# A planner that allows each weight load more time, job orders searched anew, and layer 1's rotary products on VectorE

## The chip, the cores and the metric

The kernel runs on one core of one Trainium2 chip. The metric is the device time of the whole program in microseconds, a median over runs; lower is better. Engines are named as the profile names them: PE is TensorE's matmul, PEld its weight load, DVE is VectorE, ACT is ScalarE, POOL is GpSimd, SP is SyncE, which issues the DMAs.

## The reference, cut to what matters

Two encoder layers over 256 tokens of width 1024, float32 throughout. A vector `c` gives each layer shift, scale and gate vectors through a large matrix (`w_ada`).

```python
for l in range(DEPTH):                                   # DEPTH = 2
    ada = c_act @ w_ada[l] + b_ada[l]                    # (1,1024) @ (1024,6144)
    sh1, sc1, gt1, sh2, sc2, gt2 = split(ada, 6)
    h = rms(x, g_mix[l]) * (1.0 + sc1) + sh1
    parts = split(h @ w_in[l], IN_SPLITS)                # q,k,v of A, of three groups B, two gates
    qa, ka = axial_rope(rms(qa, ..)), axial_rope(rms(ka, ..))     # rotary: x*cos + rotated(x)*sin
    y_a = gqa_attention(qa, ka, va) @ w_branch_a[l]
    qb, kb = apply_rope(rms(qb, ..)), apply_rope(rms(kb, ..))     # for each of three groups
    y_b = dilated_attention(qs, ks, vs) @ w_branch_b[l]
    mixed = sigmoid(parts[-2]) * y_a + sigmoid(parts[-1]) * y_b
    x = x + gt1 * (mixed @ w_out[l])
    h2 = rms(x, g_mlp[l]) * (1.0 + sc2) + sh2
    x = x + gt2 * (square(relu(h2 @ w_ff1[l])) @ w_ff2[l])
```

## The kernel before, in words

**Matmuls.** Each weight matrix comes in tiles of 128x1024 float32 (512 KB). A tile lands in one of six buffers `wr` (WR). ACT copies it to a rounded fp32r tile, the high part, and DVE subtracts this from the loaded tile to get the low part (`split_next`, L658); both halves together appear in the trace as `w`. The activations are split in the same way, and a product takes three matmuls: high by high, low by high, high by low (`mm3`). The tile's `wr` buffer is free again after DVE's subtraction.

**The ada jobs.** The product `c_act @ w_ada` runs on DVE alone: 96 tiles of 128x1024, each multiplied by the broadcast `c_act` and summed along its rows in one pass (`ada_tile`, L595; in the trace `s2k<-wr,c_act`, in the program's order `ISA`, followed by a row that reads the sum). A tile uses the same six `wr` buffers, and the pass frees its buffer. The jobs are spread over the kernel: 16 at the start, the `w` entries of `seq0` and `seq1` in the two mixers, and the counts in `ada_f0` and `ada_f1` between the MLP's pieces.

**Queries and keys.** The projection is made in six chunks of 512 columns (`c0` to `c5`), each for two halves `t` of the tokens. After a chunk, `qk_post` (L781) works on each half that holds queries and keys: ACT copies the PSUM bank (`qs`) and squares it (`sq`); POOL makes the rotary's second product `t2` in two instructions of 128x256 (128x64 for the keys of branch A); DVE reduces `sq`; POOL raises the sum to the power -1/2 (`rstd`); DVE makes `t1` from the bank and a table, adds `t2` and multiplies by `rstd`; PE transposes the result (`ps<-consts,s2k`). The next PE work that stands between the chunk's last matmul and these transposes is the time that this chain has: the text calls it the chain's cover.

**Other parts.** `make_h` (L716) brings the normalised and transposed tokens through shift and scale, four pieces of 128x128 at a time; `hk` says how many of the four ACT takes, and DVE takes the rest. Attention runs softmax without a further split: DVE takes the maximum, ACT the exponentials and the scaling (`pr`), PE the transposes. Gates (`u`, `v` in `seq`), branch A's projection (`y`), attention A (`a`) and B (`b`) are jobs of the mixer, in the order of `seq0` and `seq1`. `WARM` matmuls on zeros stand at PE's start.

**Order.** Nothing is issued directly. Every operation is recorded (all rows of the trace therefore carry line 549, where `Plan.issue` plays them back), and `Plan.run` plans them with fixed durations: at each step an engine takes the ready operation with the earliest due time. The plan's times are used once, to fix the order of each engine's instructions; on the chip every engine runs its own list in order and waits where an operand is late. For a load the plan takes the later of the queue's last landing and the issue plus 2100 ns, plus its bytes at a given rate:

```python
                if e == "SP":
                    b = max(pipe[0], t + 2100.0) + o["lat"] / 404.0
                    pipe[0] = b
                    end = b
```

So what the plan believes of a load decides how far behind the load its reader stands in ACT's and DVE's lists.

Of the kernel before, what the change touches and what calls it, by code (L numbers as in the profile page):

```python
# [32 lines left out]
AHEAD = 1  # L33
CFG = dict(ahead0=1, pscale="a",
  post0=(5, 2, 0, 1), s2k=7, r2k=8, ahead=1, last="k",
  dve_ss=0, hk=4,
  ada_f0=[3, 5, 3, 6, 4, 5, 1, 2, 1], ada_f1=[4, 0, 1, 0, 0, 1, 0, 0, 0],
  seq0="c3 v a w w u c4 w w w u u w w a a w w w v w w a w w v v w w w b w w w w b y w w v w y y y".split(),
  seq1="c2 u w w w c3 u c4 w w u w w v w w a w c5 u a w a w w a v b w v w w w y v y b w y w y w".split())
WR = 6  # L40
NB8 = 14
WARM = 2
PASSES = 4
HOLD = 400

# [83 lines left out]
class Plan:  # L129
# [236 lines left out]
    def run(self, due):  # L366
        ops = self.ops
        n = len(ops)
        left = [len(o["need"]) for o in ops]
        ready = [0.0] * n  # L370
        start = [None] * n
        wait = {e: [] for e in ORDERED}
        now = {e: [] for e in ORDERED}
        free = dict.fromkeys(ORDERED, 0.0)
        pipe = [1500.0]
        dve_port, held_port, last_plain = 0.0, (0.0, 0.0), False
        users = {name: len(u) for name, u in self.use.items()}
        began = {tag: 0 for tag in self.line}
        place = {name: k for names in self.line.values() for k, name in enumerate(names)}
        begun = set()  # L380
        live = dict.fromkeys(self.line, 0)
        held_by = {tag: set() for tag in self.line}
        names_of = [[f for f in sorted({z[0] for z in o["w"] + o["r"]} | set(o["also"])) if f in self.use] for o in ops]
        ev = [(0.0, 0, -1)]
        then = dict.fromkeys(ORDERED)
        state = [0]
        seen = dict.fromkeys(ORDERED)

        def fits(i):
            more = {}  # L390
            new = [z for z in names_of[i] if z not in begun]
            if not new:
                return True
            for name in sorted(new, key=lambda z: place[z]):
                tag = self.tiles[name]
                k = more[tag] = more.get(tag, 0) + 1
                if live[tag] + k > self.limit[tag]:
                    return False
                early = sum(place[z] > began[tag] for z in held_by[tag])
                if place[name] > began[tag] + k - 1:  # L400

                    if early + k + max(self.alive[tag][began[tag] : place[name]]) > self.limit[tag]:
                        return False
            return True

        for o in ops:
            if not left[o["i"]]:
                heapq.heappush(wait[o["e"]], (0.0, o["i"]))
        t = 0.0
        count = 0  # L410
        while count < n:
            moved = False
            for e in ORDERED:
                if free[e] > t:
                    continue
                w, q = wait[e], now[e]
                if then[e] is not None:
                    pick = then[e]
                    w[:] = [z for z in w if z[1] != pick]
                    q[:] = [z for z in q if z[1] != pick]  # L420
                    heapq.heapify(w)
                    heapq.heapify(q)
                else:
                    pick = None
                while w and w[0][0] <= t:
                    i = heapq.heappop(w)[1]
                    heapq.heappush(q, (due[i], i))
                    seen[e] = None
                if pick is None and seen[e] == state[0]:
                    continue  # L430
                held = []
                forced = pick is not None
                while q and not forced:
                    d, i = heapq.heappop(q)
                    if fits(i):
                        pick = i
                        break
                    held.append((d, i))
                    if len(held) > 40:
                        break  # L440
                if pick is None:
                    seen[e] = state[0]
                if pick is not None and e != "SP" and not forced:

                    end = t + ops[pick]["occ"]
                    for r, j in w:
                        if r < end and due[j] < due[pick] - self.patience and (r - t) < 0.5 * ops[pick]["occ"] and fits(j):
                            held.append((due[pick], pick))
                            pick = None
                            break  # L450
                for h in held:
                    heapq.heappush(q, h)
                if pick is None:
                    continue
                moved = True
                o = ops[pick]
                then[e] = o["then"]
                start[pick] = t
                slow = 0.0
                if e == "PE":  # L460
                    plain = o["lat"] - o["occ"] > 240
                    slow = 95.0 if last_plain and not plain else 0.0
                    last_plain = plain
                if e == "DVE" and o["port"]:
                    if held_port[0] <= t < held_port[1]:
                        slow = held_port[1] - t
                    dve_port = t + o["occ"] + slow
                elif e == "POOL" and not o["port"]:
                    slow = max(0.0, dve_port - t - 80.0)
                elif e == "POOL" and o["port"]:  # L470

                    slow = max(0.0, dve_port - t - 80.0)
                    held_port = (t, t + 80.0 + slow + 1.23 * (o["occ"] - 440.0))
                free[e] = t + o["occ"] + slow
                count += 1
                if e == "SP":
                    b = max(pipe[0], t + 2100.0) + o["lat"] / 404.0
                    pipe[0] = b
                    end = b
                else:  # L480
                    end = t + o["lat"] + slow
                heapq.heappush(ev, (free[e], 0, -1))
                heapq.heappush(ev, (end, 1, pick))
                for name in names_of[pick]:
                    if name in begun:
                        continue
                    tag = self.tiles[name]
                    live[tag] += 1
                    state[0] += 1
                    begun.add(name)  # L490
                    held_by[tag].add(name)
                    names = self.line[tag]
                    while began[tag] < len(names) and names[began[tag]] in begun:
                        began[tag] += 1
                for j, how in o["next"]:
                    left[j] -= 1
                    ready[j] = max(ready[j], end if how == 2 else t + o["occ"])
                    if not left[j]:
                        heapq.heappush(wait[ops[j]["e"]], (ready[j], j))
                        heapq.heappush(ev, (ready[j], 0, -1))  # L500
            if moved:
                continue
            assert ev, "nothing left to wait for"
            t = max(t, ev[0][0])
            while ev and ev[0][0] <= t:
                _, kind, i = heapq.heappop(ev)
                if kind:
                    for name in names_of[i]:
                        users[name] -= 1
                        if not users[name]:  # L510
                            state[0] += 1
                            live[self.tiles[name]] -= 1
                            held_by[self.tiles[name]].discard(name)
        return start, max(s + o["occ"] for s, o in zip(start, ops))
# [38 lines left out]
def encoder(ctx: ExitStack, tc: tile.TileContext, a: dict, out: bass.AP):  # L553
# [5 lines left out]
    act, dve, pool, pe, sp = plan.lanes()  # L559
# [221 lines left out]
    def qk_post(l, c, t, ps, nh, segs, axial, dst):  # L781
# [17 lines left out]
        if axial:  # L799
# [2 lines left out]
            q5, o5 = (z.rearrange("p (h b s x) -> p h b s x", b=2, s=2, x=w) for z in (qs, t2))  # L802
            sv = st[:, 0, :].rearrange("p (b s x) -> p b s x", b=2, s=2)
            for s in range(2):
                pool.tensor_tensor(
                    o5[:, :, :, s, :], q5[:, :, :, 1 - s, :],
                    sv[:, None, :, s, :].to_broadcast([P, nh, 2, w]), op=ALU.mult,
                )
        else:
            w = HD // 2  # L810
            for s in range(2):
                pool.tensor_tensor(
                    v4(t2)[:, :, :, s * w : (s + 1) * w], v4(qs)[:, :, :, (1 - s) * w : (2 - s) * w],
                    bc(st[:, :, s * w : (s + 1) * w], w), op=ALU.mult,
                )
# [615 lines left out]
```

## Time and profile before

| what | value |
|---|---|
| time, median of 3 runs | 777.55 us (776.94 to 779.17) |
| the profiled execution's own time | 781.37 us |
| its span, first to last instruction | 778.9 us |
| mean granted TensorE clock over the span | 0.987 |
| PE, share of the span busy | 96% |
| DVE, ACT, POOL | 72%, 60%, 11% |
| bytes loaded by DMA queue q1 | 179.75 MB, 65.1% of 16 engines' span |

A row of the timeline gives the start, the length, the engine, the operation, what it writes and reads and how many instructions were merged; in brackets stands the idle time of that engine just before the row, and what ended it. The profiled execution took 3.8 us more than the median of the three runs.

### The profile page before, as it was taken

The page shows a single profiled execution, that of the slowest core. Times are in us where ns is not written, and L with a number is a line of the kernel's source. Part 1 is how long each engine was busy: PE and PEld are TensorE (multiplying, and loading weights), DVE is VectorE, ACT ScalarE, POOL GpSimd, SP SyncE. Part 2 cuts the span into 40 slices and gives each one's busy share as a digit, 9 for nine tenths or more (in the row PEclk, how much of TensorE's full clock was granted, in tenths as well). Part 3 has the DMA queues.
Part 4 walks back from the last instruction along what each step waited for, and adds up shares of the span by engine and source line. Part 5 has one row for each costly group of instructions (what it writes and reads, how often), then busy time and mean ns, then how long its engine had stood idle before and what let it go on. Part 6 is the DMA issues. An engine that isn't in the chain of part 4 may idle for free.

```text
span 778.9 us, 12258 instructions
## 1 busy us (share of the span) xinstructions
PE 750.7 (96%) x4692; PEld 658.0 (84%) x4692; DVE 563.6 (72%) x805; ACT 464.0 (60%) x752; POOL 82.7 (11%) x80
## 2 busy tenths in 40 slices
PE   7998989989999999999999999989999999999998
PEld 4887878979788999998877888879887999888997
DVE  5999988879789867765378999646787955454422
ACT  7668647696357666454365646587738755555520
POOL 0007530000000014000004444000000000000000
PEclk7999999999999999999999999999999999999999
DMA  8994477957579998887334687924654975756201
GB/s 316 362 396 175 148 305 261 359 189 253 162 222 380 364 391 297 307 275 238 109 136 148 214 299 262 336 94 140 218 175 145 350 282 178 239 185 210 97 1 54
DMA packets 50393, 180.51 MB, mean 232 GB/s; under 512 B 5624, under 2 KB 6048, under 8 KB 50336
## 3 DMA queue, kind: packets, MB, share of 16 engines
q1 hardware_dynamic: 50336, 179.75, 65.1%
q8 instruction: 36, 0.59, 0.3%
q14 instruction: 21, 0.17, 0.1%
HBM read 178.66 MB, written 1.06 MB: 231 GB/s over the span
## 4 chain that ended last, share of the span: by engine, by line
PE 63%; DVE 13%; DMA 9%; ACT 8%; issue 5%; POOL 1%; SPq 0%; POOLq 0%; DVEq 0%; ACTq 0%
PE ps L549 63%; DVE s2k L549 6%; DVE w L549 4%; DMA wr<-in_w_ada 4%; ACT pr L549 3%; ACT s2k L549 2%; ACT w L549 2%; DMA wr<-in_w_gate 2%; DVE rstd L549 1%; DMA wr<-in_w_ba 1%; DMA x<-in_x 1%; DMA wr<-in_w_x 1%; DMA wr<-in_w_y 1%; DMA wr<-in_w_out 1%; DVE x L549 0%
## 5 line engine op out<-in xcount | busy, mean ns | idle before, releaser
L549 DVE TENSOR_TENSOR w<-wr,w 128x1024 fp32r<-128x1024 f32 x236 | 285.7, 1234 | 67.8 <-ACT w L549 67.1
L549 ACT ACTIVATE w<-wr 128x1024 fp32r<-128x1024 f32 x236 | 245.1, 1059 | 128.2 <-PE ps L549 63.0
L549 PE MATMUL ps<-hT,w 128*128 128x256 f32 x2112 | 272.5, 286 | 0.0
L549 PEld LDWEIGHTS ps<-hT,w 128*128 128x128 f32 x2112 | 262.6, 192 | 5.4 <-issue 3.4
L549 PE MATMUL ps<-w,r2k 128*128 128x512 f32 (+1 forms) x792 | 178.7, 385 | 0.0
L549 PEld LDWEIGHTS ps<-w,r2k 128*128 128x128 f32 x792 | 144.5, 188 | 29.5
L549 PE MATMUL ps<-w,hT 128*128 128x512 f32 x672 | 162.2, 397 | 2.8 <-ACT hT L549 1.8
L549 PEld LDWEIGHTS ps<-w,hT 128*128 128x128 f32 x672 | 125.4, 190 | 31.0 <-ACT hT L549 2.5
L549 DVE CUSTOM_DVE_ANT_0 s2k<-wr,c_act 128x1024 bf16<-128x1024 f32 x96 | 118.0, 1240 | 30.7 <-DMA wr<-in_w_ada 29.9
L549 ACT ACTIVATE s2k<-ps 128x512 f32<-128x512 f32 (+2 forms) x108 | 57.2, 562 | 68.0 <-PE ps L549 53.2
L549 POOL TENSOR_TENSOR s2k<-s2k,tabs 128x256 f32<-128x256 f32 (+1 forms) x40 | 34.2, 877 | 114.3 <-ACT s2k L549 62.6
L549 DVE TENSOR_TENSOR r2k<-s2k,r2k 128x512 fp32r<-128x512 f32 x28 | 20.1, 719 | 35.5 <-ACT r2k L549 35.5
L549 PE MATMUL ps<-w,mT 128*128 128x512 f32 x192 | 44.5, 390 | 0.0
L549 PEld LDWEIGHTS ps<-w,mT 128*128 128x128 f32 x192 | 35.8, 188 | 7.3
L549 POOL TENSOR_TENSOR ss<-ss,half 128x1 f32<-128x1 f32 x8 | 4.4, 554 | 326.1 <-DVE ss L549 326.1
L549 PE MATMUL ps<-consts,s2k 128*128 128x128 f32 x148 | 24.7, 291 | 12.0 <-DVE s2k L549 8.5
L549 ACT ACTIVATE pr<-pr,st 128x256 f32<-128x256 f32 (+1 forms) x64 | 35.5, 617 | 0.0
L549 PEld LDWEIGHTS ps<-consts,s2k 128*128 128x128 f32 x148 | 17.1, 145 | 20.1 <-DVE s2k L549 8.7
L549 POOL TENSOR_TENSOR rstd<-rstd,half 128x8 f32<-128x8 f32 (+1 forms) x20 | 33.8, 1691 | 1.1 <-DVE rstd L549 1.1
L549 PE MATMUL ps<-consts,pr 128*128 128x128 f32 x128 | 24.1, 300 | 6.2 <-ACT pr L549 6.0
L549 DVE TENSOR_TENSOR s2k<-ps,gtb 128x512 f32<-128x512 f32 (+1 forms) x18 | 11.7, 658 | 24.1 <-PE ps L549 24.1
L549 ACT ACTIVATE s2k<-x 128x512 bf16<-128x512 f32 x16 | 10.0, 627 | 31.6 <-DVE x L549 27.9
(79 smaller groups left out, 484.5 us busy)
## 6 DMA issues: line engine op xcount, KB each, us to landing
wr<-in_w_ff SPq DMA_DIRECT2D x120, 512.0 KB, 5.0
wr<-in_w_ada SPq DMA_DIRECT2D x96, 512.0 KB, 5.3
wr<-in_w_gate SPq DMA_DIRECT2D x32, 512.0 KB, 5.0
wr<-in_w_qkv SPq DMA_DIRECT2D x24, 512.0 KB, 3.8
wr<-in_w_x SPq DMA_DIRECT2D x16, 512.0 KB, 4.6
wr<-in_w_out SPq DMA_DIRECT2D x16, 512.0 KB, 4.6
wr<-in_w_y SPq DMA_DIRECT2D x8, 512.0 KB
wr<-in_w_ba SPq DMA_DIRECT2D x8, 512.0 KB, 4.8
```

The source lines that it names most:

```text
L549: getattr(self.real[o["e"]], o["op"])(*map(real, o["a"]), **{n: real(z) for n, z in o["k"].items()})
```

## The change

Five edits. The plan lets a load land 1600 ns later and at 380 instead of 404 bytes per ns. `seq0`, `seq1`, `ada_f0` and `ada_f1` hold another order of the mixers' jobs and another spread of the ada jobs (24 `w` entries in `seq0` as before, 23 instead of 20 in `seq1`, 25 instead of 30 in `ada_f0`, 8 instead of 6 in `ada_f1`). `hk` is 2, so DVE takes two of `make_h`'s four pieces. A third warm-up matmul is added. In layer 1 the rotary's second product is made by DVE.

```diff
-  dve_ss=0, hk=4,
-  ada_f0=[3, 5, 3, 6, 4, 5, 1, 2, 1], ada_f1=[4, 0, 1, 0, 0, 1, 0, 0, 0],
-  seq0="c3 v a w w u c4 w w w u u w w a a w w w v w w a w w v v w w w b w w w w b y w w v w y y y".split(),
+  dve_ss=0, hk=2,
+  ada_f0=[4, 6, 1, 6, 3, 5, 0, 0, 0], ada_f1=[3, 1, 1, 1, 2, 0, 0, 0, 0],
+  seq0="c3 a v w c4 w w w u u u w a a w w w w w w v w a w w v v w w w b w w w w w b y w w v y y y".split(),
...
-WARM = 2
+WARM = 3
...
                 if e == "SP":
-                    b = max(pipe[0], t + 2100.0) + o["lat"] / 404.0
+                    b = max(pipe[0], t + 2100.0) + o["lat"] / 380.0
                     pipe[0] = b
-                    end = b
+                    end = b + 1600.0
...
             for s in range(2):
-                pool.tensor_tensor(
+                (dve if l == 1 else pool).tensor_tensor(
                     v4(t2)[:, :, :, s * w : (s + 1) * w], v4(qs)[:, :, :, (1 - s) * w : (2 - s) * w],
```

The same edit stands in the axial branch of `qk_post`. Since the lists of all engines are planned anew, three places show what moved.

ACT's list in layer 0, up to the exponentials (`pr`) of the first pair of dilated attention; `w<-wr` is the copy of a loaded weight tile, `G` a gate. Before:

```order
L549 ACTIVATE w_173<-wr_101 128x1024
L549 ACTIVATE G_164<-ps_84 128x512
L549 ACTIVATE G_164<-G_164 128x512
L549 ACTIVATE w_174<-wr_104 128x1024
L549 ACTIVATE pr_147,st_143<-pr_147,st_143 128x512
L549 ACTIVATE pr_148,st_144<-pr_148,st_144 128x512
```

ACT's list at the same place now:

```order
L549 ACTIVATE w_172<-wr_103 128x1024
L549 ACTIVATE G_164<-ps_87 128x512
L549 ACTIVATE G_164<-G_164 128x512
L549 ACTIVATE pr_144,st_140<-pr_144,st_140 128x512
L549 ACTIVATE pr_145,st_141<-pr_145,st_141 128x512
```

The weight copy that stood directly ahead of the exponentials stands behind this pair's now; the copy ahead of the gate remains.

DVE's list in layer 0 at the first residual after the output projection (`s2k<-ps,gtb` and `x<-x,s2k`); an `ISA` row with `wr` and `c_act` is an ada job. Before:

```order
L549 TENSOR_TENSOR w_201<-wr_105,w_201 128x1024
L549 ISA s2k_75,gcol_152<-wr_100,c_act 128x1024
L549 ISA gcol_152 128x1
L549 TENSOR_TENSOR s2k_77<-ps_88,gtb_181 128x512
L549 TENSOR_TENSOR s2k_74<-ps_84,gtb_181 128x512
L549 TENSOR_TENSOR x<-x,s2k_77 128x512
L549 TENSOR_TENSOR x<-x,s2k_74 128x512
L549 ISA s2k_73,gcol_152<-wr_105,c_act 128x1024
```

DVE's list at the same place now:

```order
L549 TENSOR_TENSOR w_202<-wr_103,w_202 128x1024
L549 TENSOR_TENSOR s2k_76<-ps_83,gtb_181 128x512
L549 TENSOR_TENSOR s2k_77<-ps_84,gtb_181 128x512
L549 TENSOR_TENSOR x<-x,s2k_76 128x512
L549 TENSOR_TENSOR x<-x,s2k_77 128x512
L549 ISA s2k_78,gcol_152<-wr_104,c_act 128x1024
```

One ada job went from ahead of the residual to behind it.

DVE's list in layer 1 behind chunk `c3`, from a row of its first half to the product with `rstd` of its second half, on which the second half's transposes wait. Before:

```order
L549 TENSOR_TENSOR s2k_76<-s2k_76,s2k_79 128x512
L549 TENSOR_SCALAR rstd_129<-rstd_129 128x8
L549 ISA s2k_77,shg_97<-wr_101,c_act 128x1024
L549 ISA shg_97 128x1
L549 TENSOR_TENSOR s2k_76<-s2k_76,rstd_130 128x512
L549 TENSOR_TENSOR w_299<-wr_105,w_299 128x1024
L549 TENSOR_TENSOR s2k_73<-s2k_73,s2k_78 128x512
L549 TENSOR_TENSOR w_300<-wr_103,w_300 128x1024
L549 TENSOR_TENSOR s2k_73<-s2k_73,rstd_129 128x512
```

DVE's list at the same place now; the rows of 128x8x32 are the rotary products that POOL had:

```order
L549 TENSOR_TENSOR s2k_75<-s2k_78,tabs_257 128x8x32
L549 TENSOR_SCALAR rstd_130<-rstd_130 128x8
L549 TENSOR_TENSOR s2k_73<-ps_88,tabs_257 128x512
L549 TENSOR_TENSOR s2k_79<-s2k_79,s2k_75 128x512
L549 TENSOR_TENSOR s2k_77<-s2k_74,tabs_257 128x8x32 x2
L549 TENSOR_TENSOR s2k_79<-s2k_79,rstd_129 128x512
L549 TENSOR_TENSOR s2k_73<-s2k_73,s2k_77 128x512
L549 TENSOR_TENSOR s2k_73<-s2k_73,rstd_130 128x512
L549 TENSOR_TENSOR w_297<-wr_103,w_297 128x1024
```

Three passes over weight tiles (one ada job, two subtractions) left the chain of the two halves, and four rotary products came in (one of the four stands just above these rows). The PE list moved with it: between the second half's last matmul and its transposes stood 48 matmuls of 256 columns, 12 of 512 and 4 transposes, and now stand 46 of 256 columns and 4 transposes; for `c2` it was 48, 9 and 5 and is now 23 of 512 and 4, and for `c4` it was 72 of 256 columns and 4 and is now 22 of 512, 4 of 256 and 4. In layer 0, chunk `c4`, 43 of 256 and 6 of 512 columns stood between the first half's last matmul and its transposes, and now stand 56, 6 and 3 transposes.

Over the whole list of DVE: of the 92 ada jobs whose `wr` buffer was used before, 18 had two or fewer full-width passes of DVE (128x1024) between the pass that frees the buffer and the job itself; now 5 have.

## Rows read from the trace of the kernel before

**Rows 1.** The page's first part: busy us, share of the span, instructions.

```profile
PE 750.7 (96%) x4692; PEld 658.0 (84%) x4692; DVE 563.6 (72%) x805; ACT 464.0 (60%) x752; POOL 82.7 (11%) x80
```

**Rows 2.** Windows: PE, PEld, DVE, ACT, POOL busy; granted clock; DMA share; GB/s.

```profile
240.00:260.00 20.00, 20.00 (x126) 18.00 (x125) 18.56 (x21) 13.10 (x16) 0.00 (x0) 1.00 1.00 374
420.00:500.00 80.00, 78.35 (x457) 67.06 (x456) 73.34 (x100) 49.35 (x79) 28.51 (x24) 1.00 0.75 265
```

**Rows 3.** Timeline, layer 0, chunk c4: one row of ACT, one of PE.

```profile
105.06 1.06 ACT L549 ACTIVATE w<-wr 128x1024 fp32r<-128x1024 f32 x1 [3.11 <-DMA wr<-in_w_gate]
113.49 0.83 PE L549 MATMUL ps<-consts,s2k 128*128 128x128 f32 x4 [2.69 <-DVE s2k L549]
```

**Rows 4.** Windows: three stretches at half clock, and one behind the first.

```profile
113.80:117.20 3.40, 3.40 (x19) 3.40 (x17) 3.40 (x7) 2.34 (x4) 1.13 (x1) 0.50 0.73 269
117.20:120.60 3.40, 3.40 (x31) 3.40 (x31) 3.40 (x6) 1.03 (x2) 0.00 (x0) 0.99 0.71 247
158.20:161.60 3.40, 3.06 (x16) 2.77 (x15) 3.01 (x7) 3.02 (x7) 0.00 (x0) 0.50 0.65 225
513.20:516.60 3.40, 2.84 (x14) 2.85 (x15) 2.23 (x6) 2.75 (x9) 0.00 (x0) 0.50 0.09 12
```

**Rows 5.** Timeline, layer 0, first pair of dilated attention: ACT and PE.

```profile
151.38 1.06 ACT L549 ACTIVATE w<-wr 128x1024 fp32r<-128x1024 f32 x1 [5.46 <-DMA wr<-in_w_gate]
...
153.94 1.06 ACT L549 ACTIVATE w<-wr 128x1024 fp32r<-128x1024 f32 x1 [0.35 <-DMA wr<-in_w_ba]
...
157.78 0.55 PE L549 MATMUL ps<-consts,pr 128*128 128x128 f32 x3 [2.16 <-ACT pr L549]
```

**Rows 6.** Timeline, layer 0, residual after the output projection: DVE and PE.

```profile
200.88 1.23 DVE L549 CUSTOM_DVE_ANT_0 s2k<-wr,c_act 128x1024 bf16<-128x1024 f32 x1 [2.46 <-DMA wr<-in_w_ada]
...
206.94 0.55 PE L549 MATMUL ps<-consts,s2k 128*128 128x128 f32 x3 [1.15 <-DVE s2k L549]
```

**Rows 7.** Timeline, layer 1, three pairs of attention A: DVE's last ada job and PE.

```profile
508.59 1.23 DVE L549 CUSTOM_DVE_ANT_0 s2k<-wr,c_act 128x1024 bf16<-128x1024 f32 x1 [1.29 <-DMA wr<-in_w_ada]
...
509.74 1.88 DVE L549 TENSOR_REDUCE st<-ps 128x2 f32<-128x512 f32 x3
...
513.76 0.48 PE L549 MATMUL ps<-consts,pr 128*128 128x128 f32 x1 [3.15 <-ACT pr L549]
```

**Rows 8.** Timeline, layer 1 behind chunk c3: PE's cover, DVE's chain, the transposes.

```profile
454.09 5.91 PE L549 MATMUL ps<-hT,w 128*128 128x256 f32 x48
...
457.42 1.21 DVE L549 CUSTOM_DVE_ANT_0 s2k<-wr,c_act 128x1024 bf16<-128x1024 f32 x1
...
459.70 1.75 DVE L549 TENSOR_TENSOR w<-wr,w 128x1024 fp32r<-128x1024 f32 x1
...
461.99 1.21 DVE L549 TENSOR_TENSOR w<-wr,w 128x1024 fp32r<-128x1024 f32 x1
...
463.86 0.66 PE L549 MATMUL ps<-consts,s2k 128*128 128x128 f32 x4 [0.63 <-DVE s2k L549]
```

**Rows 9.** Timeline of PE alone, layer 0's first chunks: 512-column matmuls end to end.

```profile
47.80 16.48 PE L549 MATMUL ps<-w,hT 128*128 128x512 f32 x72
```

**Rows 10.** Groups of instructions of DVE, first 60 us: count, busy us, mean ns.

```profile
L549 DVE TENSOR_TENSOR hT<-s2k,hT 128x256 fp32r<-128x256 f32 x8 | 3.4, 423 | 0.9 <-ACT hT L549 0.8
```

**Rows 11.** Groups of instructions of POOL, 405 to 486 us: layer 1's rotary.

```profile
L549 POOL TENSOR_TENSOR s2k<-s2k,tabs 128x256 f32<-128x256 f32 x16 | 14.1, 900 | 43.5 <-ACT s2k L549 43.5
L549 POOL TENSOR_TENSOR s2k<-s2k,tabs 128x64 f32<-128x64 f32 x4 | 2.4, 624 | 0.0
```

**Rows 12.** Timeline, the start: the warm-up matmuls, and ACT's copy of c_act.

```profile
1.45 3.53 PE L549 MATMUL ps<-warm 128*128 128x512 f32 x4 [1.45 <-DVE half L549]
...
10.62 1.06 ACT L549 ACTIVATE c_act<-ps 128x512 f32<-128x512 f32 x2
```

**Rows 13.** The page's sixth part: KB each, median us from issue to landing.

```profile
wr<-in_w_ada SPq DMA_DIRECT2D x96, 512.0 KB, 5.3
```

**Rows 14.** Waits of DVE, whole span: us in total, times, longest us.

```profile
DVE s2k L549 <- DMA wr<-in_w_ada: 29.9, 22, 4.6
```

More of the change, by code (lines that the diff above doesn't have):

```diff
@@ L35 @@
   post0=(5, 2, 0, 1), s2k=7, r2k=8, ahead=1, last="k",
-  dve_ss=0, hk=4,
-  ada_f0=[3, 5, 3, 6, 4, 5, 1, 2, 1], ada_f1=[4, 0, 1, 0, 0, 1, 0, 0, 0],
-  seq0="c3 v a w w u c4 w w w u u w w a a w w w v w w a w w v v w w w b w w w w b y w w v w y y y".split(),
-  seq1="c2 u w w w c3 u c4 w w u w w v w w a w c5 u a w a w w a v b w v w w w y v y b w y w y w".split())
+  dve_ss=0, hk=2,
+  ada_f0=[4, 6, 1, 6, 3, 5, 0, 0, 0], ada_f1=[3, 1, 1, 1, 2, 0, 0, 0, 0],
+  seq0="c3 a v w c4 w w w u u u w a a w w w w w w v w a w w v v w w w b w w w w w b y w w v y y y".split(),
+  seq1="w u c2 w c3 u w w w u w w w c4 w a c5 w u a a w w a w w v b w v w w b w v w y w w v w y y y w".split())
 WR = 6
 NB8 = 14
-WARM = 2
+WARM = 3
 PASSES = 4
@@ L811, in qk_post @@
             for s in range(2):
-                pool.tensor_tensor(
+                (dve if l == 1 else pool).tensor_tensor(
                     v4(t2)[:, :, :, s * w : (s + 1) * w], v4(qs)[:, :, :, (1 - s) * w : (2 - s) * w],
```

## The prediction, made before the changed kernel was run

> **What bounds the kernel now.** I read the page's first part, then the busy time in windows, then the waits, and last the timeline around each wait of PE. The first part makes PE the bound: it is busy for 750.7 of 778.9 us, and no other engine for more than 72% [rows 1]. The windows say where this holds. In an MLP PE is busy 20.00 of 20 us at full clock [rows 2], and a change of order there can give nothing. In layer 1's mixer DVE is busy for 73.34 of 80 us, PE for 78.35 [rows 2], so the two are close to each other. What can be won are the 28 us in which PE stands idle, almost all in the start and in the mixers and residuals, and the clock that falls after the longest of those gaps.
>
> The reader should follow four gaps back to what was late. In layer 0 the transposes of chunk `c4` wait 2.69 us for DVE; eight us earlier ACT had stood 3.11 us before a gate tile's copy, with the chunk's own copies of the PSUM bank queued behind it [rows 3]. Before the first dilated pair ACT waits 5.46 us for a gate tile and 0.35 us for another tile, the exponentials stand behind both copies, and PE waits 2.16 us for them [rows 5]. At the residual DVE waits 2.46 us for an ada tile while the finished projection stands behind it, and PE waits 1.15 us [rows 6]. In layer 1 DVE waits 1.29 us for an ada tile and works 1.23 us on it, ahead of the maxima for which PE's scores were ready, and PE waits 3.15 us [rows 7]. Each is the same event: an in-order engine stands at a late load, and work that PE needs stands behind it. Loads take 5.3 us from issue to landing [rows 13], and DVE's waits for ada tiles alone sum to 29.9 us [rows 14]. Most of that costs nothing, since PE has other work; what counts is the part in those gaps.
>
> After three of them the clock falls. In the stretch behind the first gap it is granted at 0.50 (1.2 instead of 2.4 GHz), and PE starts 19 matmuls where the equally long next stretch at 0.99 has 31; behind the second and the fourth it is 0.50 as well [rows 4]. The loss is 12 of 31 starts in 3.4 us, 1.3 us each time. After the third gap of 1.15 us it does not fall.
>
> **Later readers of loads.** The lists bear out that the new plan does this: 5 ada jobs instead of 18 stand within two passes of DVE of the release of their buffer. A pass is 1.2 us [rows 8], so two passes are 2.4 us against a landing of 5.3 us. Place by place:
>
> Chunk `c4` of layer 0: the cover grows from 43 matmuls of 256 and 6 of 512 columns to 56, 6 and 3 transposes. A 256-column matmul is 5.91/48 = 0.123 us [rows 8], a 512-column one 16.48/72 = 0.229 us [rows 9], a transpose about 0.16 us (0.66/4) [rows 8]: 6.7 us become 8.7 us. Against it four passes over tiles stand in the first half's chain instead of one. I let 0.8 us of the wait stay: 2.69 + 1.3 - 0.8 = 3.2 us won; between 0 and 4.0.
>
> The dilated pair: the copy of 1.06 us and its wait of 0.35 us go from ahead of the exponentials, 1.4 us. The copy ahead of the gate stays, so a late gate tile could still hold it. With 0.8 us left of the wait the clock should hold: 1.4 + 1.3 = 2.7 us; between 0 and 3.5.
>
> The residual: the ada job with its 2.46 us is behind the residual now, and the wait of 1.15 us should go: 1.1 us.
>
> The three pairs of layer 1: the list still has an ada job directly ahead of the maxima, but with more passes between its buffer's release and itself. If the wait of 1.29 us goes, and an equal one that the pass before it can hand down does not come in its place, 3.15 becomes some 1.4 to 1.9 us. I take 1.75 us, and half of the clock's 1.3: 2.4 us; between 0 and 4.45.
>
> **Rotary on DVE.** The changed kernel takes 16 products of 128x256 and 4 of 128x64 from POOL, where they take 900 and 624 ns [rows 11]. The trace has no such product on DVE; the nearest row is DVE's 128x256 subtraction, 423 ns [rows 10]. Twenty at that price are 8.5 us, an upper bound, since four are a quarter as large; with those four at nothing it is 6.8 us. I take 7.5. What DVE gets back is read behind `c3`: with POOL at its products a subtraction takes 1.75 us, without them 1.21 us [rows 8], 0.54 us for one pass, and some three passes in each of three chunks, 4.4 us (bounds 0 and 6). Three more ada jobs in layer 1's mixer are 3 x 1.23 = 3.7 us. So DVE's load there rises by 7.5 - 4.4 + 3.7 = 6.8 us, and 80 - 73.34 = 6.7 us are free: DVE is just full. The chain itself gets shorter: it takes 463.86 - 454.09 = 9.8 us from the second half's last matmul to the transposes, with three passes of 1.21, 1.75 and 1.21 us in it that are gone from there, and four products of 0.42 us come in: 9.8 - 4.2 + 1.7 - 1 (passes no longer lengthened) = 6.3 us. Its cover falls from 9.3 us to 46 x 0.123 + 4 x 0.16 = 6.3 us, so that place stays even with its wait of 0.63 us [rows 8]. For the full DVE I put a loss of 1.5 us, between 0 and 6.8.
>
> By the Trainium skill (SBUF, "Who interferes with whom") the two engines share a port pair, which one instruction holds in full while the other blocks; the trace agrees in kind, with a lengthening of 0.54 us beside POOL instructions of 0.9 us. Another page of it (Perfetto Trace Analysis, "Optimizing Scalar/DVE Operations") speaks against the edit: where DVE is saturated, work should rather be taken off it, though an exchange between these two engines may not help. By the lock alone DVE would get back 20 x 0.9 us less its own 7.5, a gain; by the other page the stretch would be lost as in the second rival below; here the trace stands between them.
>
> **Edits at nothing.** The third warm-up matmul adds two rows of 3.53/4 = 0.88 us [rows 12], and PE's next work, the broadcast of `c`, ends some 1.8 us later; ACT takes its result at 10.62 us, after other work [rows 12], with about 3 us to spare. Uncovered it would cost 1.8 us, and a clock that stays up longer could give about as much back; 0. `hk` gives DVE 24 pieces, at most 0.42 us each [rows 10], four or eight together behind a residual, and takes as many from ACT; PE is then at the rest of the projection or the first MLP matmuls. Uncovered: 4 x 0.42 = 1.7 us at each of six places, less what ACT saves; 0.
>
> **New waits.** Every list is new, so some readers will be late in places that had no wait. I put two of the third gap's size, 2 x 1.1 = 2.2 us, between 0 and 6.
>
> **The sum.** -3.2 - 2.7 - 1.1 - 2.4 + 1.5 + 2.2 = -5.7 us. The profiled execution took 781.37 us, so the same conditions would show 775.7; it stands 3.8 us over the median of the runs, 777.55, from which the forecast is 771.8 us.
>
> **The rivals.** First, more is won: all four waits go with their three half-clock stretches (2.69 + 2.16 + 1.15 + 3.15 + 3 x 1.3 = 13.0) and nothing new comes: 764.5 us. For it: one event explains all four. Against it: softmax and `c4` keep a tight cover.
>
> Second, and on the other side, DVE becomes the bound in layer 1. The place is the three chains behind `c2`, `c3`, `c4`, whose cover falls by 3.0 us each (for `c2` 48 x 0.123 + 9 x 0.229 + 5 x 0.16 = 8.8 to 23 x 0.229 + 0.6 = 5.9). If the chain of the second half does not get shorter, each transposes' wait grows by 3.0 us, to a length after which the clock fell elsewhere: 3 x (3.0 + 1.3) = 12.9 us, and with the -7.2 us of the other terms (-9.4 + 2.2) that is +5.7: 783 us. It decides from a chain of more than about 6.3 us; the trace has 9.8 now. For it: DVE is full there by my own sum. Against it: three foreign passes have visibly left the chain.
>
> Third, the waits only change places: PE has cover for most of DVE's 29.9 us already, and the new lists trade those four gaps for others of the same sum: 777.5 us, no change.
>
> **How the numbers follow.** My forecast has 0.55, its own range 766 to 776; more won 0.14; no change 0.15; DVE bound 0.16. About 0.3% (2.3 us) is what a measurement of this kernel can tell from no change. Faster than that: 0.14 and nine tenths of 0.55, 0.64. Within it: 0.15 and a twentieth from the forecast's upper end, 0.20. Slower: 0.16. The range for 8 in 10 leaves out the lower half of the first rival and the upper part of the second: 762 to 780 us.
>
> **What would show it.** Right: no PE wait over 1 us before the transposes of layer 0's `c4`, none at its residual, fewer stretches at clock 0.50 between 100 and 520 us, and DVE's waits for ada tiles well under 29.9 us. In layer 1's mixer, rotary products of 0.35 to 0.42 us on DVE, no more subtractions of 1.75 us, and DVE busy over 75 of 80 us with PE waits under 1 us behind `c2` to `c4`. Wrong: waits of 2 us or more at those transposes, or as many half-clock stretches at other places as were there before.

## The result and the profile after

The changed kernel takes 766.24 us (median of 4 runs, 765.16 to 767.65) against 777.25 us (4 runs, 776.89 to 779.17) for the kernel before: ratio 0.9855, 95% interval 0.9831 to 0.9878. That is 11.0 us faster, where 5.7 had been forecast. The profiled execution took 765.16 us, 1.1 us below its median; that of before stood some 4 us above its own, so the two profiles are 16.2 us apart.

The page's first part (as [rows 1]), and the window from 100 to 520 us, in which the three half-clock stretches of [rows 4] lay (columns as [rows 2]):

```profile
PE 746.6 (98%) x4694; PEld 650.9 (85%) x4694; DVE 571.8 (75%) x849; ACT 456.3 (60%) x728; POOL 68.8 (9%) x60
```

```profile
100.00:520.00 420.00, 413.57 (x2706) 363.22 (x2706) 337.55 (x515) 262.67 (x437) 33.50 (x25) 1.00 0.70 253
```

PE stands idle for 17 us of 763.4 instead of 28, and none of the windows of 3.4 us in that stretch has a granted clock below 1.00. The waits, whole span (us, times, longest us), the last line as [rows 14]:

```profile
PE ps L549 <- DVE s2k L549: 2.0, 4, 0.6
PE ps L549 <- ACT pr L549: 1.3, 3, 0.6
DVE s2k L549 <- DMA wr<-in_w_ada: 1.0, 1, 1.0
```

DVE's 29.9 us before ada tiles are 1.0 us. PE waited 8.5 us for `s2k` and 6.0 us for `pr` before, up to 3.1 us at a time; in this execution no such wait is over 0.6 us now. The four gaps, in the timeline: layer 0's `c4` (as [rows 3]), the dilated pair (as [rows 5]), the residual (as [rows 6]) and layer 1's attention A (as [rows 7]):

```profile
103.66 1.06 ACT L549 ACTIVATE w<-wr 128x1024 fp32r<-128x1024 f32 x1 [4.08 <-DMA wr<-in_w_gate]
...
104.75 0.60 PE L549 MATMUL ps<-consts,s2k 128*128 128x128 f32 x4
...
109.50 0.60 PE L549 MATMUL ps<-consts,s2k 128*128 128x128 f32 x4
...
141.94 1.06 ACT L549 ACTIVATE w<-wr 128x1024 fp32r<-128x1024 f32 x1 [2.15 <-DMA wr<-in_w_gate]
...
148.18 0.55 PE L549 MATMUL ps<-consts,pr 128*128 128x128 f32 x3
...
192.38 1.22 DVE L549 CUSTOM_DVE_ANT_0 s2k<-wr,c_act 128x1024 bf16<-128x1024 f32 x1
...
194.88 0.55 PE L549 MATMUL ps<-consts,s2k 128*128 128x128 f32 x3
...
494.74 0.33 PE L549 MATMUL ps<-consts,pr 128*128 128x128 f32 x1 [0.57 <-ACT pr L549]
```

At `c4` ACT still stands 4.08 us before a gate tile, longer than the 3.11 of before. But nothing that PE needs is queued behind it any more: the copies of the chunk's banks come before it, and the transposes of both halves find their operands. The other three gaps are gone or 0.57 us long.

Layer 1 behind `c3` (as [rows 8]), and DVE's groups in layer 1's mixer, which bear on the rotary ([rows 11] had POOL's):

```profile
443.39 5.20 PE L549 MATMUL ps<-hT,w 128*128 128x256 f32 x42
...
446.97 0.76 DVE L549 TENSOR_TENSOR s2k<-s2k,tabs 128x256 f32<-128x256 f32 x2
...
449.88 0.63 PE L549 MATMUL ps<-consts,s2k 128*128 128x128 f32 x4 [0.36 <-DVE s2k L549]
```

```profile
L549 DVE CUSTOM_DVE_ANT_0 s2k<-wr,c_act 128x1024 bf16<-128x1024 f32 x23 | 27.5, 1219 | 1.0 <-DMA wr<-in_w_ada 1.0
L549 DVE TENSOR_TENSOR s2k<-s2k,tabs 128x256 f32<-128x256 f32 x16 | 6.4, 420 | 0.9 <-ACT s2k L549 0.7
...
L549 DVE TENSOR_TENSOR s2k<-s2k,rstd 128x512 f32<-128x512 f32 x8 | 5.5, 685 | 0.2
L549 DVE TENSOR_TENSOR s2k<-s2k,tabs 128x64 f32<-128x64 f32 x4 | 0.7, 218 | 0.0
```

Where the 15.5 us between the two spans came from is read from the starts of PE's groups of matmuls:

| stretch | before, us | after, us | difference |
|---|---|---|---|
| to the first product (`ps<-w,hT`) | 17.5 | 15.0 | -2.5 |
| to the first dilated scores, `c4` included | 132.8 | 128.4 | -4.4 |
| dilated attention, to branch B's projection | 33.5 | 29.7 | -3.8 |
| branch B, output projection, residual | 30.5 | 29.4 | -1.1 |
| to the end of layer 0's MLP | 184.6 | 185.3 | +0.7 |
| layer 1's mixer, to branch B | 163.1 | 159.4 | -3.7 |
| the rest, to the end of the last matmul | 213.1 | 212.4 | -0.7 |

The second row holds more than `c4`. The kernel before has a fifth gap in it, in layer 0's first chunks, which the prediction leaves out although it is longer than the one at the residual. DVE's chain there had waited for a rotary product of POOL (0.63 us), not for a load. The changed kernel has no wait at its transposes there:

```profile
73.86 0.63 PE L549 MATMUL ps<-consts,s2k 128*128 128x128 f32 x4 [1.69 <-DVE s2k L549]
```

### The profile page after: what moved, and what is told of

It reads as the page before. It is cut to its first block, busy times and chain, and to the rows that moved or that the text cites. A ratio compares the mean times of both kernels' runs of the same rounds, so it can differ in the third digit from the quotient of the medians.

```text
span 763.4 us, 12235 instructions
## 1 busy us (share of the span) xinstructions
PE 746.6 (98%) x4694; PEld 650.9 (85%) x4694; DVE 571.8 (75%) x849; ACT 456.3 (60%) x728; POOL 68.8 (9%) x60
## 4 chain that ended last, share of the span: by engine, by line
PE 76%; ACT 10%; DVE 8%; issue 3%; DMA 2%; SPq 0%; POOL 0%; ACTq 0%; DVEq 0%
PE ps L549 76%; DVE s2k L549 4%; ACT pr L549 4%; ACT s2k L549 3%; DVE w L549 2%; ACT w L549 2%; DMA wr<-in_w_x 2%; DMA x<-in_x 1%; DVE hT L549 1%; DVE rstd L549 1%; ACT G L549 0%; ACT hT L549 0%; ACT qk L549 0%; DVE pr L549 0%; ACT xT L549 0%
## 5 line engine op out<-in xcount | busy, mean ns | idle before, releaser
L549 PE MATMUL ps<-hT,w 128*128 128x256 f32 x2112 | 269.0, 285 | 0.0
L549 PEld LDWEIGHTS ps<-hT,w 128*128 128x128 f32 x2112 | 259.7, 191 | 5.5 <-issue 2.4
L549 PEld LDWEIGHTS ps<-w,hT 128*128 128x128 f32 x672 | 123.6, 188 | 32.6 <-ACT hT L549 4.6
L549 PEld LDWEIGHTS ps<-consts,s2k 128*128 128x128 f32 x148 | 16.4, 140 | 13.5 <-ACT s2k L549 4.8
L549 POOL TENSOR_TENSOR s2k<-s2k,tabs 128x256 f32<-128x256 f32 (+1 forms) x20 | 21.2, 1081 | 56.8 <-ACT s2k L549 49.8
L549 PE MATMUL ps<-oa,w 128*128 128x256 f32 x192 | 24.7, 285 | 0.0
```

The costliest lines, as they stand in the source:

```text
L549: getattr(self.real[o["e"]], o["op"])(*map(real, o["a"]), **{n: real(z) for n, z in o["k"].items()})
```

## The experiments

Times are medians, ratios are to the kernel before, timed beside each kernel. Its median was 776.31 to 779.75 us beside the different groups of kernels, so between tables the ratio is the safer number.

### One edit alone, on the kernel before

Theory A said that late readers of loads are the gain, so that the planned load time should carry it alone. The rivals were that the job order carries it, or that the rotary on DVE or the clock does.

```diff
 e1, one warm-up more, all lists kept as planned with two:
+                reps = 2 if o["e"] == "PE" and not warmed else 1
 e2:
-                    b = max(pipe[0], t + 2100.0) + o["lat"] / 404.0
+                    b = max(pipe[0], t + 2100.0) + o["lat"] / 380.0
-                    end = b
+                    end = b + 1600.0
 e3: ada_f0, ada_f1, seq0 and seq1 of the change
 e4:
-                pool.tensor_tensor(
+                (dve if l == 1 else pool).tensor_tensor(
```

> The kernel before, every list kept as it was, with only one more warm-up matmul played at PE's head. If the start's clock carries part of the 11.0 us, the first product matmul comes at about 15.0 us instead of 17.5, no stretch at clock 0.50 is left before 25 us, and the time is 1.5 to 4 us below the kernel before. By the prediction's own term (nothing) it is 777 within 1 us.

> The kernel before with only the plan's load time changed (1600 ns later, 380 instead of 404 bytes per ns), planned anew. If late readers of loads carry the gain: 5 to 8 us below the kernel before, so 769 to 772, and DVE's waits for ada tiles fall from 29.9 to under 15 us. If the new job order carries it: 776 to 778.

> The kernel before with only the new job order and spread of ada jobs, planned anew with the old load time. If late readers of loads carry the gain: 775 to 779, with DVE's waits for ada tiles near 30 us. If the job order carries it: 770 to 772.

> The kernel before with only layer 1's rotary products on DVE, planned anew. By the prediction's sum (DVE just full, chain a little shorter) 776 to 779; if the port that DVE shares with POOL cost much, 773 to 775; if DVE becomes the bound in layer 1, 780 to 784, with waits of 2 us and more at layer 1's transposes.

| kernel | us | ratio, interval | DVE's wait for ada tiles, us |
|---|---|---|---|
| e1, third warm-up | 775.95 | 0.9983, 0.9959 to 1.0006 | 33.8 |
| e2, load time | 770.86 | 0.9929, 0.9904 to 0.9954 | 6.6 |
| e3, job order | 779.80 | 1.0033, 1.0014 to 1.0052 | 23.4 |
| e4, rotary on DVE | 779.49 | 1.0034, 1.0013 to 1.0055 | 33.2 |

The load time alone wins 0.7%, about half of the change or more, and lies where theory A put it. The job order and the rotary, put alone into the kernel before, cost 0.3% each; both times lie just above the range expected for them. The warm-up is worth nothing that can be told, at most 0.4% by its interval.

### One edit taken out of the changed kernel

```diff
 e5, one warm-up fewer, all lists kept as planned with three:
+                if o["e"] == "PE" and not warmed:
 e6:
-                    b = max(pipe[0], t + 2100.0) + o["lat"] / 380.0
+                    b = max(pipe[0], t + 2100.0) + o["lat"] / 404.0
-                    end = b + 1600.0
+                    end = b
 e7: ada_f0, ada_f1, seq0 and seq1 of before
 e8:
-                (dve if l == 1 else pool).tensor_tensor(
+                pool.tensor_tensor(
```

> The changed kernel, every list kept, with only the third warm-up matmul left out. If the start's clock carries part of the gain, stretches at clock 0.50 come back before 25 us and the time is 1.5 to 4 us above the changed kernel, 768 to 770. If it carries nothing: 766 within 1 us.

> The changed kernel with the plan's old load time (404 bytes per ns, no 1600 ns), planned anew. If late readers of loads carry the gain: 771 to 775, and DVE's waits for ada tiles rise to 25 us and more. If not: 765 to 768.

> The changed kernel with the old job order and old spread of ada jobs, planned anew with the new load time. If the load time carries the gain: 767 to 769. If the job order does: 771 to 775.

> The changed kernel with layer 1's rotary products back on POOL, planned anew. By the prediction's sum (a loss of 1.5 us through a full DVE) 764 to 766; if the edit wins by the shared port, 768 to 770.

| kernel | us | ratio, interval | DVE's wait for ada tiles, us |
|---|---|---|---|
| e5, two warm-ups | 767.78 | 0.9851, 0.9828 to 0.9874 | 1.2 |
| e6, old load time | 774.31 | 0.9931, 0.9912 to 0.9949 | 18.1 |
| e7, old job order | 767.25 | 0.9838, 0.9818 to 0.9858 | 3.6 |
| e8, rotary on POOL | 766.29 | 0.9821, 0.9800 to 0.9843 | 0.9 |

Of these four only the load time is missed, by 6.5 to 8 us against its three neighbours. With the old load time waits of the old kind are back, those of DVE (whole span; 18.1 us, fewer than the 25 expected) and those of PE:

```profile
DVE s2k L549 <- DMA wr<-in_w_ada: 18.1, 14, 2.9
PE ps L549 <- DVE s2k L549: 7.7, 11, 1.7
```

e8 also prices the rotary. Layer 1's mixer there in the windows (columns as [rows 2]), and the groups of DVE that stand beside POOL's work:

```profile
388.50:548.40 159.90, 155.88 (x1037) 134.10 (x1036) 130.53 (x207) 105.50 (x196) 33.40 (x31) 1.00 0.67 232
```

```profile
L549 DVE CUSTOM_DVE_ANT_0 s2k<-wr,c_act 128x1024 bf16<-128x1024 f32 x23 | 28.2, 1241 | 0.8 <-DMA wr<-in_w_ada 0.8
L549 DVE TENSOR_TENSOR s2k<-s2k,rstd 128x512 f32<-128x512 f32 x8 | 7.3, 917 | 0.4 <-POOL rstd L549 0.4
```

and the same stretch of the changed kernel:

```profile
387.60:547.20 159.60, 155.68 (x1037) 134.22 (x1036) 132.63 (x227) 105.45 (x196) 16.12 (x11) 1.00 0.65 232
```

The products cost DVE 6.4 + 0.7 = 7.1 us, yet its busy time rises by only 2.1 us, from 130.53 to 132.63: 5.0 us come back, since its passes are no longer lengthened beside POOL's (the multiplication by `rstd` takes 685 instead of 917 ns, 1.8 us in all; the rest is spread over other groups). The stretch itself has the same length within 0.3 us.

### The remainder

e2 leaves open where the rest of the 11 us is, since none of the other edits tried so far wins anything alone. `hk` was still untried.

```diff
 e9, on the kernel before; e10 the reverse on the changed kernel:
-  dve_ss=0, hk=4,
+  dve_ss=0, hk=2,
 e11: e2 and e9 together
```

> The kernel before with hk=2 alone: DVE takes two of the four pieces of shift and scale, ACT the other two. Theory A, hk carries the part of the gain that the load time does not: ratio 0.991 to 0.995, like the changed kernel with the old load time (0.9931), with the first product and the first rows of the MLPs earlier. Theory B, hk is worth nothing (the prediction's term of 0) and the rest of the gain is an interaction of the edits or the luck of one plan among many: ratio 0.998 to 1.004, as the job order and the rotary had alone.

> The changed kernel with hk=4 again. Theory A: it gives back 4 to 6 us, ratio 0.990 to 0.993. Theory B: ratio 0.982 to 0.988, as the changed kernel itself.

> The kernel before with the load time and hk=2, but the old job order, the rotary on POOL and two warm-ups. Theory A, these two edits are the whole change: ratio 0.980 to 0.988, as good as the changed kernel or better. Theory B: ratio 0.990 to 0.995, as the load time alone (0.9929); what is left to the changed kernel then needs another order as well.

`hk` alone: 776.63 us, 0.9975 (0.9952 to 0.9998), at most half a per cent. The changed kernel without it: 767.31 us, 0.9868 (0.9850 to 0.9885), not to be told from the changed kernel. Load time and `hk`: 770.26 us, 0.9908 (0.9893 to 0.9923). The second and third are theory B, and the first lies just below its range: the two edits are not the whole change, and 3 to 4 us of it are still missing. So each of the other three edits was added to e11, and the changed kernel was planned with 100 ns less, to see whether its list is one lucky draw:

```diff
 e13: e11 with ada_f0, ada_f1, seq0 and seq1 of the change
 e14: e11 with
-                pool.tensor_tensor(
+                (dve if l == 1 else pool).tensor_tensor(
 e15: e11 with
-WARM = 2
+WARM = 3
 e16: the changed kernel with
-                    end = b + 1600.0
+                    end = b + 1500.0
```

> The kernel before with the load time, hk=2 and the new job order (rotary on POOL, two warm-ups). Theory A, the order pays only once loads are planned late enough, because it moves chains clear of the waits that the load time leaves: ratio 0.982 to 0.986, level with the changed kernel. Theory B, the order is worth nothing here either: 0.989 to 0.993, as without it (0.9908).

> The kernel before with the load time, hk=2 and layer 1's rotary products on DVE (old order, two warm-ups). Theory A, order and rotary are two ways to the same 3 us: ratio 0.983 to 0.987, and the waits of PE behind chunks c2 to c4 of layer 1 (0.59, 0.80 and 0.78 us more than PE's usual pace without it) fall by half or more. Theory B: 0.989 to 0.993.

> The kernel before with the load time, hk=2 and a third warm-up that the plan knows of, so that all lists are planned from a PE that is free 1.8 us later. If it is the plan's start that makes the rest of the gain: ratio 0.982 to 0.986, with the first product 1.5 us earlier (15 instead of 16.6 us). If it is worth nothing, as the played one was: 0.989 to 0.993.

> The changed kernel with 1500 instead of 1600 ns, a change too small to mean anything for a load of 5 us, which still lets the plan fall out differently. If the gain is the later readers, the ratio stays at 0.983 to 0.988. If the order was searched for just these numbers and its gain is that of one lucky plan, it falls back to 0.989 to 0.995.

| kernel | us (range) | ratio, interval |
|---|---|---|
| e13, with order | 766.89 (766.19 to 767.09) | 0.9883, 0.9867 to 0.9900 |
| e14, with rotary | 767.85 (765.53 to 767.94) | 0.9887, 0.9868 to 0.9907 |
| e15, with third warm-up | 767.61 (767.17 to 767.63) | 0.9890, 0.9876 to 0.9905 |
| e16, changed, 1500 ns | 766.34 (764.61 to 767.96) | 0.9875, 0.9852 to 0.9897 |

The kernel before ran at 776.31 us beside these four, lower than beside the others, so the ratios stand higher than the times suggest. e16 has the changed kernel's time, so the list is no single lucky draw. In times, each of e13 to e15 takes another 2.4 to 3.4 us off e11 (769.72 to 770.51 us); in ratios the intervals overlap with that of e11, and the three ratios lie between the two theories or at the edge of the second, so the size of this last step is not settled. Where it stands is told by the stretches, read as in the table of the result:

| kernel | to first product | to dilated scores | dilated attention | B to residual | layer 1's mixer |
|---|---|---|---|---|---|
| before | 17.5 | 132.8 | 33.5 | 30.5 | 163.1 |
| e2, load time | 15.5 | 128.7 | 30.0 | 29.2 | 163.2 |
| e6, changed, old load time | 15.3 | 128.2 | 30.9 | 32.6 | 164.7 |
| e11, load time and `hk` | 16.6 | 128.7 | 30.0 | 29.2 | 162.0 |
| e13, with order | 15.2 | 128.3 | 30.2 | 29.4 | 159.6 |
| e14, with rotary | 16.1 | 129.5 | 30.0 | 29.2 | 159.6 |
| e15, with third warm-up | 14.6 | 128.8 | 30.0 | 29.2 | 161.0 |
| changed | 15.0 | 128.4 | 29.7 | 29.4 | 159.4 |

The load time alone (e2) brings layer 0's stretches to where the changed kernel has them, and leaves layer 1's mixer as it was. There the wait for `pr` falls from 3.15 to 0.90 us, and a new one has come at the transposes behind `c4`:

```profile
470.97 0.66 PE L549 MATMUL ps<-consts,s2k 128*128 128x128 f32 x4 [2.47 <-DVE s2k L549]
```

With everything but the load time (e6) the residual and layer 1's mixer are longer than before. So the mixer's gain takes the load time and another edit. In e11 its waits stand behind `c3` and `c4` and at a transpose of exponentials:

```profile
452.37 0.66 PE L549 MATMUL ps<-consts,s2k 128*128 128x128 f32 x4 [0.61 <-DVE s2k L549]
470.93 0.66 PE L549 MATMUL ps<-consts,s2k 128*128 128x128 f32 x4 [0.62 <-DVE s2k L549]
504.73 0.33 PE L549 MATMUL ps<-consts,pr 128*128 128x128 f32 x1 [1.50 <-ACT pr L549]
```

and the same in e14:

```profile
452.94 0.63 PE L549 MATMUL ps<-consts,s2k 128*128 128x128 f32 x4 [0.23 <-DVE s2k L549]
502.58 0.33 PE L549 MATMUL ps<-consts,pr 128*128 128x128 f32 x1 [0.69 <-ACT pr L549]
```

With the rotary on DVE (e14) or the new order (e13) layer 1's mixer is 2.5 and 2.4 us shorter than in e11: these two are ways to the same few waits. With the planned third warm-up (e15) 1.0 us is won there and 2.0 us before the first product. The three do not add up: the changed kernel has all and is level with any one.

### How much time a load should get

```diff
 e17, e18, e12, on the changed kernel:
-                    end = b + 1600.0
+                    end = b + 800.0
+                    end = b + 2400.0
+                    end = b + 3200.0
```

> The changed kernel with loads planned 800 instead of 1600 ns later (rate 380 as there). If the gain grows with the time given: about half way between the old load time in this kernel (774.3 us) and the changed kernel (766.2), 769 to 772 us, and DVE waits for ada tiles between 3 and 18 us in all. If a small margin is enough: 765 to 768.

> The changed kernel with 2400 ns. If the best lies above 1600 ns: 763 to 766 us, the version that beats both. If 3200 ns was bad because every reader moves back and DVE's due work piles up, part of that loss shows here: 768 to 772. If 3200 ns was bad by one unlucky list, 2400 stays at 765 to 768.

> The changed kernel with loads planned 3200 instead of 1600 ns later. If the gain goes with the time given, and readers are still late at 1600 ns (DVE's remaining 3 us of waits for ada tiles), the ratio is 0.980 to 0.984. If 1600 ns already covers the landing, nothing is left to win, and later readers only keep buffers longer, so that loads are issued later: 0.985 to 0.990. If a list made at random near this one is what counts, it can land anywhere from 0.982 to 0.995.

| added to a load, ns | us | ratio, interval | DVE's wait for ada tiles, us |
|---|---|---|---|
| 0, at 404 bytes per ns (e6) | 774.31 | 0.9931, 0.9912 to 0.9949 | 18.1 |
| 800 (e17) | 770.96 | 0.9903, 0.9878 to 0.9927 | 8.7 |
| 1500 (e16) | 766.34 | 0.9875, 0.9852 to 0.9897 | 2.5 |
| 1600 (changed) | 766.24 | 0.9855, 0.9831 to 0.9878 | 1.0 |
| 2400 (e18) | 773.50 | 0.9933, 0.9909 to 0.9958 | 1.0 |
| 3200 (e12) | 774.91 | 0.9966, 0.9953 to 0.9978 | 0.8 |

Up to 1500 or 1600 ns, which the runs do not tell apart, the time falls with the wait for the tiles. Above, that wait stays at 1 us and the time rises by 7 to 9 us: a second cost takes over, at 2400 and at 3200 ns a larger one than any of the cases expected for them. In e18 it stands in two stretches: 134.6 instead of 128.4 us to the first dilated scores, and 33.1 instead of 29.7 us in the dilated attention. The windows of e18 show the first in layer 0's first chunks:

```profile
60.00:100.00 40.00, 35.29 (x187) 27.07 (x186) 36.00 (x59) 28.15 (x61) 22.20 (x22) 0.96 0.43 144
```

The changed kernel has PE busy for 39.57 of these 40 us, and the DMA share at 0.49. PE's timeline with 3200 ns (e12), and then that of the changed kernel at the same transposes:

```profile
62.66 0.73 PE L549 MATMUL ps<-w,hT 128*128 128x512 f32 x2 [0.73 <-ACT v L549]
66.97 1.12 PE L549 MATMUL ps<-consts,s2k 128*128 128x128 f32 x4 [3.58 <-DVE s2k L549]
```

```profile
59.67 7.24 PE L549 MATMUL ps<-w,hT 128*128 128x512 f32 x30
67.06 0.63 PE L549 MATMUL ps<-consts,s2k 128*128 128x128 f32 x4
```

PE starts 2 matmuls between a first stop of 0.73 us and the transposes, for which it then waits 3.58 us; in the changed kernel matmuls run on without a stop, 30 in the row shown. That the plan lacked ready work there because it thought the weights were still to come is argued from the lists and was not tested by itself.

## Why the prediction was half right

The mechanism was right for layer 0, and the sum failed at two terms that stood against the gain: the loss of 1.5 us for a full DVE and the 2.2 us for new waits. Together they are 3.7 of the 5.3 us by which the gain was put too low; the other part is waits that went further than the prediction allowed. The time, 766.24 us, lies in the range, 0.2 us above the lower end of the likeliest case's own range and nearer to the first rival (764.5) than to the forecast (771.8). The rival to which I gave 0.14 described it better: all four waits go, or nearly, with their half-clock stretches, and in the profiled execution nothing new of any size comes.

**The cause.** Later readers of loads carry it: e2 wins 6.9 us with the load time alone, e6 shows that the changed kernel cannot do without it, and from 0 to 1600 ns the time falls with DVE's wait for tiles. In layer 1's mixer they are not enough. There the load time alone shortens the wait that the prediction had traced, but another wait comes instead, and the stretch keeps its length.

**`c4`, dilated pair, residual (-3.2, -2.7, -1.1).** The stretches shrank by 4.4, 3.8 and 1.1 us. The 0.8 us that I left of each of the first two waits did not stay: no wait did. But the 4.4 us hold the fifth gap of 1.69 us as well, which I had not seen, and `c4`'s wait does not need the load time: it is gone in e6 too, and 0.81 us in e3. The one at the dilated pair went beyond my upper bound of 3.5 us, which counted the one gap; other waits of that stretch went as well.

**Layer 1's mixer (-2.4 and +1.5).** It shrank by 3.7 us where I had a net 0.9. The wait of 3.15 us, of which I left some 1.4, became 0.57. The loss for the full DVE did not come. Its parts were nearly right: rotary products 7.1 us (forecast 7.5), given back 5.0 us (forecast 4.4), the time from the second half's last matmul behind `c3` to its transposes 449.88 - 443.39 = 6.5 us (forecast 6.3). The step that failed is "DVE is just full". I took 80 us of the mixer, its fullest half, and put all of the added load there. Over the whole mixer DVE's busy time rose from 125.35 to 132.63 us, 7.3 where I had 6.8 (1.5 of the 7.3 are pieces of `hk`, which I had left out), but to 83% of 159.6 us only, and the new lists put the added work elsewhere. The matching 80 us of the changed kernel are less full than the 73.34 of before, not over 75 as my sign of being right had it:

```profile
409.00:489.00 80.00, 78.58 (x456) 66.97 (x455) 71.97 (x115) 47.75 (x77) 13.10 (x8) 1.00 0.70 257
```

The changed kernel with and without the edit (e8) cannot be told apart. By the Trainium skill (Perfetto Trace Analysis, "Optimizing Scalar/DVE Operations") moving work between DVE and GpSimd might not help. The runs agree where the edit is put into the kernel before (0.3% slower) or taken out of the changed one (766.29 against 766.24 us); beside the load time and `hk` (e14) it may have helped.

**New waits (+2.2).** The second failed step. Every list was new, so I put in two new gaps without naming a place or a cause. The stretches outside the four places moved by +0.7 and -0.7 us, and the longest new wait of PE in the changed kernel's profile is 1.22 us, at 22.03 us. That is in part luck. Neighbours of the changed kernel do have such a gap in layer 1's mixer: 2.47 us in e2, and 1.9 us in e5, e10 and e16, of which e5 plays the changed kernel's own lists less one warm-up. In e5 it is not a late load: POOL takes 5.48 us for two `rstd` passes, against 3.61 us in the changed kernel, and DVE and then PE wait for it. What lengthened them is open:

```profile
433.83 5.48 POOL L553 TENSOR_TENSOR rstd<-rstd,half 128x8 f32<-128x8 f32 x2 [14.11 <-DVE rstd L553]
440.19 0.63 PE L553 MATMUL ps<-consts,s2k 128*128 128x128 f32 x4 [1.94 <-DVE s2k L553]
```

```profile
432.29 3.61 POOL L549 TENSOR_TENSOR rstd<-rstd,half 128x8 f32<-128x8 f32 x2 [14.10 <-DVE rstd L549]
437.23 0.63 PE L549 MATMUL ps<-consts,s2k 128*128 128x128 f32 x4 [0.52 <-ACT qk L549]
```

**Edits at nothing.** Right for the warm-up as played (e1, e5) and nearly for `hk` (0.9975 alone; no difference that can be told in the changed kernel). The first product comes 2.5 us earlier than in the profile of before, whose clock was 0.50 from 8.0 to 14.8 us. Some of this is the warm-up's: with one fewer in the same lists (e5) the first product comes at 16.4 instead of 15.0 us, and planned beside e11's edits (e15) the third one brings it forward by 2.0 us. The played one does not show in the time (e1, e5). The rest is the difference between two executions and belongs to the 5.2 us by which the profiles differ more than the medians.

**The other rivals.** DVE did not become the bound behind `c2` to `c4` (783): PE waits at most 0.6 us there. The waits did not change places (777.5) at 1600 ns; they do so in part with the load time alone, in layer 1's mixer, and at 2400 and 3200 ns, where the loads are in time and PE lacks cover instead.

**What stays open.** Which of order, rotary or planned warm-up takes the last 2.4 to 3.4 us in the changed kernel: any one of them does, and two kernels that differ only in the plan's numbers can differ by as much. No version tried is faster than the changed kernel by more than the runs can tell.

## What to carry to other kernels

Where a plan fixes each engine's order and the engines run in order, the plan's belief on when a load lands is a tuning knob with two sides: too early and readers stand at the head of a queue, too late and the bound engine has no ready work to cover the chains. Sweep it, since here 800 ns to either side cost 0.5% and 0.8%. A term for new waits needs a place and a cause, or it belongs in the range and not in the sum; and judge whether an engine gets full over the whole stretch in which its work can move, not over its fullest part.

## What was not expected of the hardware

A weight tile's wait can grow and cost nothing: ACT's stop before a gate tile went from 3.11 to 4.08 us at the place where PE's wait of 2.69 us vanished.

The granted clock of a window can read 1.00 where PE runs at about half pace. In e5 it reads 1.00 over the first 20 us. Yet eight transposes at its start take 1.97 us, as long as at a granted clock of 0.50 in the kernel before, while in the changed kernel they take 1.09 us. The rows are of e5, of before and of the changed kernel:

```profile
8.88 1.97 PE L553 MATMUL ps<-consts,s2k 128*128 128x128 f32 x8
```

```profile
12.35 1.97 PE L549 MATMUL ps<-consts,s2k 128*128 128x128 f32 x8
```

```profile
9.11 1.09 PE L549 MATMUL ps<-consts,s2k 128*128 128x128 f32 x8
```

So at the start the length of the matmuls tells the pace. Three warm-ups do not always keep it up: e7, which plays three as the changed kernel does, has a granted clock of 0.50 from 9.7 to 13.1 us. Each of these is one execution.
